# Last FFN: seven block products in group 10 as well, x added from DRAM onto the gated sum, adaLN tiles at a rate of each group until group 6, h of a group in one slot

## The chip, the cores and the metric

The kernel runs on one core of a Trainium2 chip. The metric is the time of one execution on the device in microseconds (us). Times of single instructions come from a hardware profile of one execution.

## What is computed

One residual block with three sublayers: an FFN at half weight, a mixer (mLSTM and RG-LRU heads), and a second FFN at half weight. Each has a modulation of its input and a gate that come from adaLN, the product of silu(c) and a weight matrix. The change lies in the third sublayer.

```python
def _swiglu(u, w13, w2):
    g, v = jnp.split(u @ w13, 2, axis=-1)
    return (jax.nn.silu(g) * v) @ w2
...
        mod = (jax.nn.silu(c) @ w_ada[l] + b_ada[l]).reshape(B, N_SUBLAYERS, 3, D_MODEL)
        shift, scale, gate = mod[:, :, 0], mod[:, :, 1], mod[:, :, 2]
...
        y = _swiglu(modulate(x, 2), ffn2_w13[l], ffn2_w2[l])
        x = _layer_norm(ALPHA * x + FFN_WEIGHT * gate[:, 2, None, :] * y, ln_g[l, 2], ln_b[l, 2])
```

x is 256 tokens by 2048 columns, the FFN is 5632 wide, everything is float32, and ALPHA is the fourth root of 2.

## The kernel before

**Weights.** Every weight tile is 128 partitions by 2048 columns, 1 MB, loaded by SyncE's queue into one of four raw buffers. `split` (called by `load_w`) makes a high half by a cast on ScalarE (ACT) and a low half by a subtraction on VectorE (DVE), line 110, three buffers each. A product is three passes: high by high, high by low, low by high. `mov_t` issues it for one tile and one half of the tokens as 12 matmuls of 128x512 on TensorE (PE), and `mov_w` for both halves, 24 matmuls.

**The last FFN** goes over 11 blocks of 512 columns of the FFN, 0 to 10. Blocks 0, 1 and 10 are made by `rows_block`: four weight tiles for g, four for v, 24 matmuls each. Blocks 2 to 9 (`FAST`) are made by `fast_block`: half of the inner dimension is taken with seven block products in place of eight, after Strassen and Winograd, from sums of the weight tiles that DVE makes (line 756, 761, 766 and 775) and from sums of the activations that `sums` makes once. Its 15 parts of 12 matmuls stand in place of 16. Between the parts it takes four `x_tile` steps, the products of the group before with w2, which are added to `yacc` by DVE (line 745). `turn_one` transposes the silu product of a block and makes its high and low half (h). `closing` makes the last w2 products and the last layer norm.

**x** is spilled to DRAM (`xd`) by `sums`, since its buffer is wanted for the sums of the activations. `restore` reads it back behind block 9 and multiplies it by ALPHA on ACT, and `residual` (lines 334 and 335) multiplies yacc by the gate and adds it onto x, on DVE, while block 10 runs.

**adaLN.** Every weight tile load calls `tick`, which adds a rate to a credit, and for each full credit one adaLN tile is loaded (1 MB into a raw buffer) and reduced by one operation on DVE, line 210. In the last FFN the rate is 0.5 and the credit starts at -2. Sixteen tiles, 128 to 143, give the gate of this sublayer; `gate_rows` turns them, writes them to DRAM and reads them back over all partitions with a DMA from GpSimd (POOL), line 234.

**Order.** A scheduler fixes the order of each engine's instructions when the program is built, and each engine takes its own in that order. An instruction waits until what it reads is there and the buffer that it writes is free, and everything behind it on its engine waits with it.

Names: the banks of a fast block are `fa`, `fb`, `fc` and `fd`; `py` is a bank for w2 products; `lfw` and `hfw` are the low and high halves of w13 tiles, `lw` and `hw` of w2 tiles; tile 20q is the second sum of block 2's tile 0 (a p, q or r behind the number marks a sum); `u` and `n` at the mixer's end are the modulated input of the last FFN, `tu` its transposed form, `sh`, `hf` and `lf` halves of its first weights.

Of the kernel before, what the change touches and what calls it, by code (L numbers as in the profile page):

```python
# [16 lines left out]
P = 128  # L17
# [24 lines left out]
FFN2_RATE = 0.5  # L42
# [3 lines left out]
FAST = range(2, 10)  # L46


class Held:
# [9 lines left out]
def block_kernel(ctx: ExitStack, tc: tile.TileContext, a: dict, out: bass.AP):  # L59
# [594 lines left out]
    def ffn(s, w13, w2, start, following=None):  # L654
# [8 lines left out]
        b0 = RAMP // 4 if start else 0  # L663
# [5 lines left out]
        def rows_block(b, passed=None):  # L669

            i = 8 * (b - b0)
            if passed:
                pg, pv = passed[0], met(passed, w13[4:8], f"fv{s}")
            else:
                pg = [bank(f"fg{s}{b}{t}") for t in range(NT)]
                for k in range(4):
# [4 lines left out]
                for k in range(4):
                    mov_w(pv, load_w(w13[i + 4 + k], f"fv{s}_{b}{k}"), uh, ul, k * 4, k == 0, k == 3)
# [5 lines left out]
        def sums():  # L688

            nc.gpsimd.dma_start(xd, x.tile)  # L690
            f = raw_tile("sums").rearrange("p (a b) -> p a b", b=P)
            for t in range(NT):
                tk = slice(t * P, (t + 1) * P)
                nc.vector.tensor_add(f[:, 8 * t:8 * t + 8, :], uh[:, 0:8, tk].bitcast(F32), ul[:, 0:8, tk].bitcast(F32))
            a11, a12, a21, a22 = (f[:, 4 * i:4 * i + 4, :] for i in range(4))
            nc.vector.tensor_add(a22, a21, a22)
            nc.vector.tensor_sub(a21, a11, a21)
            nc.vector.tensor_sub(a11, a22, a11)
            nc.vector.tensor_sub(a12, a12, a11)
            both = big.tile([P, 2, KT, P], F32R, tag="x", name="ws")  # L700
            nc.scalar.copy(both[:, 0], f)
            nc.vector.tensor_sub(both[:, 1], f, both[:, 0].bitcast(F32))
            return both[:, 0], both[:, 1]

        def restore():
            x.tile = tokens("x1")
            for t in range(NT):
                nc.gpsimd.dma_start(x[:, t, :], xd[:, t, :])
            scale_x()

        def fast_block(b, wh, wl):

            i = 8 * b
            gi = 4 * b // GRP - 1
            s2_, s4_, s3_, s1_ = 0, 4, 8, 12
            p1, p5 = bank(f"fa{b}"), bank(f"fb{b}")
            py = {}

            def part(ps, hl, h, k0, t, first, last):
                return mov_t(ps, hl, *h, k0, t, first, last, T, skip_group_check=not first and ps in (p1, p5))  # L720

            def fresh(k, row=False):
                return load(w13[i + k], f"fw{s}_{b}{k}", None, row_tile(f"fw{b}{k}") if row else None)

            def halves(tile, w=""):
                return split((tile[0], tile[1] + w, None), nc.scalar, nc.vector)

            def kept(ps, tag, w):
                to = sm.tile([P, 512], F32, tag=tag, bufs=2, name=f"{w}{s}{b}")
                nc.scalar.copy(to, ps)  # L730
                return to

            def x_tile(m):
                n, k = b % 2 * 2 + m // 2, m % 2
                if not k:
                    py[n] = [bank(f"py{gi}_{n}_{t}") for t in range(NT)]
                kg = 2 * gi + k
                end = mov_w(py[n], load_w(w2[kg * 4 + n], f"w2{s}_{kg}_{n}"), *hts[gi], k * 4, not k, k == 1, T)
                if k:
                    c = slice(n * 512, (n + 1) * 512)  # L740
                    for t in range(NT):
                        if gi == 0:
                            evac.append(nc.scalar.copy(yacc[t][:, c], py[n][t]))
                        else:
                            nc.vector.tensor_add(yacc[t][:, c], yacc[t][:, c], py[n][t])
                return end

            u, w = (uh, ul), (wh, wl)
            ta = fresh(0, True)
            end = part(p1, halves(ta), u, 0, 0, True, True)  # L750
            turn_one(end)
            f1 = kept(p1, "u", "fs")
            tc_ = fresh(4, b >= 4)
            end = x_tile(0)
            turn_one(end)
            nc.vector.tensor_sub(ta[0], tc_[0], ta[0])
            part(p5, halves(ta, "p"), w, s1_, 0, True, True)
            f5 = kept(p5, "gy", "ft")
# [337 lines left out]
        if not following:  # L1096
            return
# [461 lines left out]
```

## Time and profile before

| | us |
|---|---|
| median of 3 runs | 1883.9 |
| lowest and highest run | 1880.34, 1885.63 |
| the profiled execution | 1882.46 |
| its span | 1880.7 |
| PE busy | 1861.4 |
| DVE busy | 1561.3 |
| ACT busy | 895.1 |

The profile belongs to one execution, so that sums of its rows are to be set against 1882.46 and not against the median. Matmuls overlap: a row of PE gives 0.39 us for one, and the time from one start to the next is 0.23 us. A row of the timeline gives in brackets how long its engine stood idle ahead of the instruction, and what ended that. Group 10 of the title is block 10.

### The profile page before, as it was taken

The page shows a single profiled execution, that of the slowest core. Times are in us where ns is not written, and L with a number is a line of the kernel's source. Part 1 is how long each engine was busy: PE and PEld are TensorE (multiplying, and loading weights), DVE is VectorE, ACT ScalarE, POOL GpSimd, SP SyncE. Part 2 cuts the span into 40 slices and gives each one's busy share as a digit, 9 for nine tenths or more (in the row PEclk, how much of TensorE's full clock was granted, in tenths as well). Part 3 has the DMA queues.
Part 4 walks back from the last instruction along what each step waited for, and adds up shares of the span by engine and source line. Part 5 has one row for each costly group of instructions (what it writes and reads, how often), then busy time and mean ns, then how long its engine had stood idle before and what let it go on. Part 6 is the DMA issues. An engine that isn't in the chain of part 4 may idle for free.

```text
span 1880.7 us, 21240 instructions
## 1 busy us (share of the span) xinstructions
PE 1861.4 (99%) x8495; PEld 1526.0 (81%) x8495; DVE 1561.3 (83%) x1467; ACT 895.1 (48%) x847; POOL 43.2 (2%) x68
## 2 busy tenths in 40 slices
PE   8999999999999999999999999999999999999998
PEld 5788888888888888788888887878778888888886
DVE  6899998887887987889997877789887788778776
ACT  4543444533334335756644356454544455545441
POOL 0000000000000000100000121000000000000000
PEclk9999999999999999999999999999999999999999
DMA  9989889999899987478687574768855654564662
GB/s 377 417 354 366 319 311 347 357 348 355 344 357 355 339 331 269 148 276 296 244 317 296 203 264 182 268 246 300 307 210 190 224 212 168 202 224 186 239 224 90
DMA packets 74931, 520.06 MB, mean 277 GB/s; under 512 B 8736, under 2 KB 8912, under 8 KB 13520
## 3 DMA queue, kind: packets, MB, share of 16 engines
q1 hardware_dynamic: 72144, 507.54, 71.6%
q0 software_dynamic: 960, 7.37, 1.0%
q10 hardware_dynamic: 1728, 3.80, 0.6%
q8 instruction: 66, 1.08, 0.2%
q14 instruction: 33, 0.27, 0.0%
HBM read 514.46 MB, written 4.22 MB: 276 GB/s over the span
## 4 chain that ended last, share of the span: by engine, by line
PE 92%; DVE 4%; DMA 2%; issue 1%; ACT 1%; POOL 0%; POOLq 0%; DVEq 0%; SPq 0%; ACTq 0%
PE py L133 9%; PE pj L281 5%; PE fa L133 5%; PE fb L133 4%; PE fc L133 3%; PE fd L133 3%; PE py L293 3%; PE py L294 3%; PE py L292 3%; PE pj L283 3%; PE fg L293 3%; PE fg L294 3%; PE fg L292 3%; PE fv L293 3%; PE fv L292 3%; PE fv L294 3%
## 5 line engine op out<-in xcount | busy, mean ns | idle before, releaser
L210 DVE CUSTOM_DVE_ANT_0 ada<-ada,scb,badac 128x2048 f32<-128x2048 f32 x110 | 258.0, 2345 | 39.5 <-DMA ada<-in_w_ada 39.0
L108 ACT CAST hw<-rw 128x2048 fp32r<-128x2048 f32 x81 | 155.1, 1914 | 218.0 <-DMA rw<-in_w 60.6
L110 DVE TENSOR_TENSOR lw<-rw,hw 128x2048 fp32r<-128x2048 f32 x81 | 185.1, 2287 | 55.8 <-ACT hw L108 55.0
L110 DVE TENSOR_TENSOR lfw<-rfw,hfw 128x2048 fp32r<-128x2048 f32 x48 | 109.9, 2289 | 17.2 <-ACT hfw L108 17.2
L281 PE MATMUL pj<-u,hs 128*128 128x512 f32 x512 | 122.5, 391 | 0.0
L108 ACT CAST hra<-rra 128x2048 fp32r<-128x2048 f32 x38 | 72.6, 1914 | 102.2 <-DMA rra<-in_w_r 43.1
L108 ACT CAST hfw<-rfw 128x2048 fp32r<-128x2048 f32 x48 | 91.9, 1915 | 47.8 <-PE py L133 28.2
L281 PEld LDWEIGHTS pj<-u,hs 128*128 128x128 f32 x512 | 94.3, 188 | 18.4
L133 PE MATMUL py<-lw,hth 128*128 128x512 f32 x256 | 99.8, 390 | 2.1 <-DVE lw L110 2.1
L133 PE MATMUL py<-hw,hth 128*128 128x512 f32 x256 | 100.4, 392 | 0.0
L293 PE MATMUL py<-lw,hth 128*128 128x512 f32 x256 | 99.8, 390 | 0.1
L294 PE MATMUL py<-hw,htl 128*128 128x512 f32 x256 | 99.7, 390 | 0.0
L133 PE MATMUL py<-hw,htl 128*128 128x512 f32 x256 | 99.7, 389 | 0.0
L292 PE MATMUL py<-hw,hth 128*128 128x512 f32 x256 | 97.3, 392 | 0.0
L108 ACT CAST hfg<-rfg 128x2048 fp32r<-128x2048 f32 x28 | 53.6, 1914 | 86.1 <-DMA rfg<-in_w 48.8
L108 ACT CAST hs<-rs 128x2048 fp32r<-128x2048 f32 x32 | 61.0, 1908 | 68.7 <-PE pj L281 53.6
L293 PE MATMUL fg<-lfg,u 128*128 128x512 f32 x224 | 87.4, 390 | 0.1
L294 PE MATMUL fg<-hfg,u 128*128 128x512 f32 x224 | 87.3, 390 | 0.0
L293 PE MATMUL fv<-lfv,u 128*128 128x512 f32 x224 | 87.2, 389 | 0.0
L294 PE MATMUL fv<-hfv,u 128*128 128x512 f32 x224 | 87.1, 389 | 0.0
L108 ACT CAST hfv<-rfv 128x2048 fp32r<-128x2048 f32 x28 | 53.6, 1913 | 66.7 <-DMA rfv<-in_w 41.3
L292 PE MATMUL fg<-hfg,u 128*128 128x512 f32 x224 | 84.5, 392 | 0.0
(727 smaller groups left out, 4764.4 us busy)
## 6 DMA issues: line engine op xcount, KB each, us to landing
ada<-in_w_ada SPq DMA_DIRECT2D x138, 1024.0 KB, 6.5
rw<-in_w SPq DMA_DIRECT2D x81, 1024.0 KB, 5.5
rfw<-in_w SPq DMA_DIRECT2D x50, 1024.0 KB, 4.8
rra<-in_w_r SPq DMA_DIRECT2D x45, 1024.0 KB, 7.4
rs<-in_w_s SPq DMA_DIRECT2D x32, 1024.0 KB, 5.0
rfg<-in_w SPq DMA_DIRECT2D x28, 1024.0 KB, 6.7
rfv<-in_w SPq DMA_DIRECT2D x28, 1024.0 KB, 5.5
rwo<-in_w_out SPq DMA_DIRECT2D x16, 1024.0 KB, 4.8
```

The lines of the kernel that those rows point to most:

```text
L108: act.copy(cut(hi, w), like(raw[:, w], hi))
L110: low.tensor_sub(cut(lo, w), like(raw[:, w], lo), cut(hi, w).bitcast(F32))
L133: self.last = getattr(self.engine, op)(*args, **kw)
L210: vec.tensor_tensor_reduce(raw[:, c], raw[:, c], scb[:, c], 1.0, base, ALU.mult, ALU.add, to)
L281: nc.tensor.matmul(ps, hi[:, k * P:(k + 1) * P], both(k), start=k == 0, stop=False)
L283: nc.tensor.matmul(ps[:, 0:S], lo[:, k * P:(k + 1) * P], uh[:, k, :], start=False, stop=k == KT - 1)
L292: pe.matmul(o, acth[:, k0 + j, tk], cut(hi, w), start=first and j == 0, stop=False, **kw)
L293: pe.matmul(o, acth[:, k0 + j, tk], cut(lo, w), start=False, stop=False, **kw)
L294: end = pe.matmul(o, actl[:, k0 + j, tk], cut(hi, w), start=False, stop=last and j == 3, **kw)
```

## The change

`last_ffn` is a function of its own, and `ffn` serves the first FFN alone. In it:

- Blocks 2 to 10 are fast blocks. `fast_block` follows a plan, a list of steps: S4 for blocks 2 to 9, S2 for block 10, whose two w2 steps are the first two of the closing products. The signs of the sums are others, so that c - a, -a - d and a + b are made one after the other in the buffer of a, and c + d in that of c. In before a sum of b and a was made in the buffer of b.
- x is multiplied by ALPHA ahead of its spill. It isn't read back: when block 9 is done, yacc is multiplied by the gate in place, and two DMAs from POOL add xd onto yacc, which is x from there on.
- adaLN runs at a rate of its own for each block (0.5, 0.5, 0.17, 0.3, 0.3, 0.3 for blocks 0 to 5) from a credit of 0, and what is left is done ahead of block 6. From block 6 to 9 tile c takes a buffer of the two that the vector c of adaLN and the gate use; before it did from block 4 on.
- h is kept for each block in one slot, high and low half together; before, for each group of two blocks in two slots.

```diff
-FFN2_RATE = 0.5
+FFN2_RATE = (0.5, 0.5, 0.17, 0.3, 0.3, 0.3)
...
-FAST = range(2, 10)
...
+ADA_END = 6
...
-            credit[:] = -2.0, FFN2_RATE
-            rows_block(0, nxt.pop())
-            rows_block(1)
-            ws = sums()
-            for b in FAST:
-                fast_block(b, *ws)
-            restore()
-            done = FAST.stop // 2 - 1
...
+                elif w == "P5":
+                    W["c", q] = fresh(q, 4, not DOUBLE and ADA_END <= b < n_b - 1)
+                    a, c = W["a", q], W["c", q]
+                    vec.tensor_sub(a[0], c[0], a[0])
+                    hl = halves(a, "p")
...
+                elif w == "P6":
+                    a = W["a", q]
+                    d = W["d", q] = fresh(q, 5, q == 1)
+                    vec.scalar_tensor_tensor(a[0], a[0], -1.0, d[0], op0=ALU.mult, op1=ALU.subtract)
+                    hl = halves(a, "q")
...
+                elif w == "P7":
+                    c, d = W["c", q], W["d", q]
+                    if not dma:
+                        vec.tensor_add(c[0], c[0], d[0])
...
+                elif w == "P4":
+                    a = W["a", q]
+                    if not dma:
+                        vec.tensor_add(a[0], a[0], W["b", q][0])
+                    normal("4", halves(a, "r"), u, ku + 4, 1)
...
+        credit[:] = 0.0, FFN2_RATE[0]
+        rows_block(0, nxt.pop())
+        rows_block(1)
+        for t in range(NT):
+            nc.scalar.mul(x[:, t, :], x[:, t, :], ALPHA)
+        nc.gpsimd.dma_start(xd, x.tile)
+        ws = [sums(0, in_x)]
+        S4 = "P1 t X t P5 X P6 P3 X P7 P2 G P4 G X V".split()
+        S2 = "P1 t G t P5 X P6 P3 G P7 P2 X P4 V".split()
...
+        gate_rows(s, 0.5)
+        for t in range(NT):
+            for n in range(4):
+                c = slice(n * 512, (n + 1) * 512)
+                nc.vector.tensor_mul(yacc[t][:, c], yacc[t][:, c], gate[:, c])
+            nc.gpsimd.dma_start(yacc[t], xd[:, t, :], accum_op=ALU.add)
+        x.tile = yacc
...
+        fast_block(n_b - 1, ws[:1], begun(), S2)
```

**How it moves the order.** ACT at the end of the mixer, before: the modulated input (`u`, `n`) is made from its transposed form, token half 0.

```order
L133 ACTIVATE n_8253<-x_113,nbn_8250,rsn_8248 128x512
L133 ACTIVATE u_0_8273<-tu_0_8258,adac 128x128 x4
L133 ACTIVATE u_1_8300<-tu_1_8264,adac 128x128 x4
L133 CAST u_114<-u_1_8300 128x4x128
L133 ACTIVATE n_8253<-tu_2_8290,adac 128x128 x4
L133 ACTIVATE n_8253<-tu_3_8295,adac 128x128 x4
```

ACT at the same place in the change:

```order
L138 ACTIVATE n_8253<-x_113,nbn_8250,rsn_8248 128x512
L138 ACTIVATE u_0_8273<-tu_0_8258,adac 128x128 x4
L1164 ACTIVATE x_113<-x_113 128x2048
L138 ACTIVATE u_1_8300<-tu_1_8264,adac 128x128 x4
L138 CAST u_114<-u_1_8300 128x4x128
L138 ACTIVATE n_8253<-tu_2_8290,adac 128x128 x4
L138 ACTIVATE n_8253<-tu_3_8295,adac 128x128 x4
```

The multiplication of x's first half (L1164) stands between the two pieces of u; that of the second half stands in the same way ahead of the first piece of u for the second half.

DVE behind that, where the low half of the FFN's first weights is made (`lf`), before:

```order
L133 TENSOR_TENSOR u_114<-u_3_8470,u_114 128x4x128
L133 TENSOR_TENSOR lf_8496<-rf_8362,hf_8495 128x512 x4
L133 TENSOR_TENSOR u_114<-n_8253,u_114 128x4x128 x2
L110 TENSOR_TENSOR lfv2b_8541<-rfv2b_8538,hfv2b_8540 128x2048
L110 TENSOR_TENSOR lfv2b_8571<-rfv2b_8568,hfv2b_8570 128x2048
L110 TENSOR_TENSOR lfv2b_8601<-rfv2b_8598,hfv2b_8600 128x2048
L210 ISA ada_8705,adac<-ada_8705,scb,badac 128x2048
```

And in the change:

```order
L138 TENSOR_TENSOR u_114<-u_3_8470,u_114 128x4x128
L215 ISA ada_8566,adac<-ada_8566,scb,badac 128x2048
L215 ISA adac 128x1
L138 TENSOR_TENSOR lf_8496<-rf_8362,hf_8495 128x512 x4
L138 TENSOR_TENSOR u_114<-n_8253,u_114 128x4x128 x2
L115 TENSOR_TENSOR lfv2b_8539<-rfv2b_8536,hfv2b_8538 128x2048
L115 TENSOR_TENSOR lfv2b_8572<-rfv2b_8569,hfv2b_8571 128x2048
L215 ISA ada_8637,adac<-ada_8637,scb,badac 128x2048
```

The first adaLN operation (ISA ada) has moved ahead of `lf_8496`, and the second ahead of the third `lfv2b`.

DVE in block 3 from the low half of its second sum on, before:

```order
L110 TENSOR_TENSOR lfw_30q<-fw_9348,hfw_30q 128x2048
L110 TENSOR_TENSOR lfw_35_9498<-rfw_35_9441,hfw_35_9497 128x2048
L210 ISA ada_9566,adac<-ada_9566,scb,badac 128x2048
L210 ISA adac 128x1
L110 TENSOR_TENSOR lw_0_3_9518<-rw_0_3_9515,hw_0_3_9517 128x2048
L110 TENSOR_TENSOR lfw_34q<-rfw_34_9378,hfw_34q 128x2048
L110 TENSOR_TENSOR lfw_31_9572<-rfw_31_9569,hfw_31_9571 128x2048
L775 TENSOR_TENSOR rfw_31_9569<-rfw_31_9569,fw_9348 128x2048
```

And in the change:

```order
L115 TENSOR_TENSOR lfw_30q<-fw_30_9340,hfw_30q 128x2048
L115 TENSOR_TENSOR lfw_35_9490<-rfw_35_9468,hfw_35_9489 128x2048
L1132 TENSOR_TENSOR fw_30_9340<-fw_30_9340,rfw_31_9556 128x2048
L115 TENSOR_TENSOR lw_0_3_9510<-rw_0_3_9507,hw_0_3_9509 128x2048
L115 TENSOR_TENSOR lfw_34q<-rfw_34_9411,hfw_34q 128x2048
L115 TENSOR_TENSOR lfw_31_9559<-rfw_31_9556,hfw_31_9558 128x2048
L215 ISA ada_9623,adac<-ada_9623,scb,badac 128x2048
```

The adaLN operation has left the place ahead of the w2 tile `lw_0_3`, and the sum a + b (L1132), which was line 775 behind `lfw_31`, has come there.

DVE from the end of block 9 into block 10, before:

```order
L110 TENSOR_TENSOR lfw_97_12160<-rfw_97_12157,hfw_97_12159 128x2048
L745 TENSOR_TENSOR yacc_8509<-yacc_8509,py_3_0_11967 128x512
L745 TENSOR_TENSOR yacc_8510<-yacc_8510,py_3_1_11968 128x512
L110 TENSOR_TENSOR lfg_100_12256<-rfg_100_12253,hfg_100_12255 128x2048
L792 TENSOR_TENSOR fv_11949<-fv_11949,fb_11810 128x512
L793 TENSOR_TENSOR fs_11836<-fs_11836,fv_11949 128x512
L334 TENSOR_TENSOR gy_12227<-yacc_8509,gate_12225 128x512
L335 TENSOR_TENSOR x_12215<-x_12215,gy_12227 128x512
L334 TENSOR_TENSOR gy_12230<-yacc_8509,gate_12225 128x512
L335 TENSOR_TENSOR x_12215<-x_12215,gy_12230 128x512
```

And in the change:

```order
L115 TENSOR_TENSOR lfw_97_12161<-rfw_97_12158,hfw_97_12160 128x2048
L1035 TENSOR_TENSOR yacc_8954<-yacc_8954,py_3_0_11968 128x512
L1035 TENSOR_TENSOR yacc_8955<-yacc_8955,py_3_1_11969 128x512
L1188 TENSOR_TENSOR yacc_8954<-yacc_8954,gate_12221 128x512 x4
L1188 TENSOR_TENSOR yacc_8955<-yacc_8955,gate_12221 128x512 x4
L115 TENSOR_TENSOR lfw_100_12237<-fw_100_12233,hfw_100_12236 128x2048
L1148 TENSOR_TENSOR f_11950<-f_11950,f_11884 128x512
L1092 TENSOR_TENSOR fw_100_12233<-rfw_104_12301,fw_100_12233 128x2048
L1157 TENSOR_TENSOR f_11828<-f_11828,f_11950 128x512
L115 TENSOR_TENSOR lfw_102_12265<-rfw_102_12262,hfw_102_12264 128x2048
L1149 TENSOR_TENSOR f_11897<-f_11897,f_11811 128x512
L1121 TENSOR_TENSOR rfw_104_12301<-rfw_104_12301,rfw_105_12355 128x2048
```

The eight products by the gate stand in a row ahead of the low half of block 10's first tile, and two sums of weight tiles (L1092, L1121) follow.

## Rows read from the trace of the kernel before

**Rows 1.** The page, part 1: busy time, share of the span and instructions of each engine.

```profile
PE 1861.4 (99%) x8495; PEld 1526.0 (81%) x8495; DVE 1561.3 (83%) x1467; ACT 895.1 (48%) x847; POOL 43.2 (2%) x68
```

**Rows 2.** What PE waits for, 1230 to 1881: us in total, times, longest.

```profile
PE fa L133 <- DVE lfw_20q L110: 2.6, 1, 2.6
PE py L133 <- DVE lw L110: 2.1, 2, 1.3
```

**Rows 3.** Busy time by stretch; columns in the first line.

```profile
core 0: us, PE busy (x) PEld busy (x) DVE busy (x) ACT busy (x) POOL busy (x), PEclk, DMA share, GB/s
1242.00:1300.00 58.00, 55.42 (x241) 45.06 (x240) 51.38 (x33) 30.58 (x24) 0.00 (x0) 0.97 0.74 274
...
1509.00:1576.00 67.00, 67.00 (x301) 55.50 (x300) 53.99 (x35) 34.75 (x26) 0.00 (x0) 1.00 0.55 201
```

**Rows 4.** Timeline of PE: start, duration, engine, line, instruction, [idle before, releaser].

```profile
1257.78 0.39 PE L133 MATMUL py<-hw,htl 128*128 128x512 f32 x1
...
1260.05 0.39 PE L133 MATMUL fa<-hfw_20q,ws 128*128 128x512 f32 x1
1263.02 0.50 PE L133 MATMUL fa<-lfw_20q,ws 128*128 128x512 f32 x1 [2.58 <-DVE lfw_20q L110]
...
1267.16 0.47 PE L133 MATMUL fb<-hfw,ws 128*128 128x512 f32 x1
...
1324.44 0.50 PE L133 MATMUL py<-lw,hth 128*128 128x512 f32 x1 [0.77 <-DVE lw L110]
```

**Rows 5.** Busy time around the wait at 1263; columns as in rows 3.

```profile
1262.50:1267.20 4.70, 4.18 (x12) 3.27 (x13) 4.70 (x3) 0.13 (x1) 0.00 (x0) 0.65 0.68 234
```

**Rows 6.** Timeline of ACT, the two multiplications of x.

```profile
1745.59 3.71 ACT L133 ACTIVATE x<-x 128x2048 f32<-128x2048 f32 x2
```

**Rows 7.** Timeline of ACT at the end of the mixer.

```profile
1149.64 2.90 ACT L133 ACTIVATE u<-tu,adac 128x128 f32<-128x128 f32 x8 [0.47 <-PE tu L133]
1152.58 0.62 ACT L133 CAST u<-u 128x512 fp32r<-128x512 f32 x1
...
1162.81 1.50 ACT L133 ACTIVATE u<-tu,adac 128x128 f32<-128x128 f32 x4 [0.43 <-PE tu L133]
1164.35 0.62 ACT L133 CAST u<-u 128x512 fp32r<-128x512 f32 x1
```

**Rows 8.** Timeline of PE at the end of the mixer.

```profile
1153.25 0.50 PE L133 MATMUL f<-sh,u 128*128 128x512 f32 x1
...
1165.56 0.47 PE L133 MATMUL f<-hf,u 128*128 128x512 f32 x1
...
1177.00 0.39 PE L293 MATMUL f<-lf,u 128*128 128x512 f32 x1
```

**Rows 9.** Timeline of DVE: an adaLN operation, and lf.

```profile
1258.40 2.35 DVE L210 CUSTOM_DVE_ANT_0 ada<-ada,scb,badac 128x2048 f32<-128x2048 f32 x1 [2.08 <-DMA ada<-in_w_ada]
...
1175.43 2.49 DVE L133 TENSOR_TENSOR lf<-rf,hf 128x512 fp32r<-128x512 f32 x4
```

**Rows 10.** Timeline of DVE from the end of block 9 on.

```profile
1747.93 1.35 DVE L745 TENSOR_TENSOR yacc<-yacc,py 128x512 f32<-128x512 f32 x2
...
1762.15 2.28 DVE L110 TENSOR_TENSOR lfg<-rfg,hfg 128x2048 fp32r<-128x2048 f32 x1
1764.36 0.68 DVE L335 TENSOR_TENSOR x<-x,gy 128x512 f32<-128x512 f32 x1
1764.96 0.68 DVE L793 TENSOR_TENSOR fu<-fu,ft 128x512 f32<-128x512 f32 x1
```

**Rows 11.** DMA issues, 1130 to 1881: KB each, median us to landing.

```profile
xd<-x POOLq DMA_DIRECT2D x1, 2048.0 KB, 11.1
...
gate<-rowd POOLq DMA_DIRECT2D x1, 1024.0 KB, 8.3
```

**Rows 12.** Busy time in block 10; columns as in rows 3.

```profile
1759.28:1802.80 43.52, 43.52 (x197) 36.08 (x196) 31.91 (x30) 19.17 (x13) 0.00 (x0) 1.00 0.54 194
```

**Rows 13.** Timeline of POOL, the gate's transfer.

```profile
1742.98 0.56 POOL L234 DMA_DIRECT2D gate<-rowd  x1 [5.26 <-DVE lfw L110]
```

More of the change, by code (lines that the diff above doesn't have):

```diff
@@ L54, in __getitem__ @@
     def __getitem__(self, key):
+        if isinstance(self.tile, list):
+            p, t, c = key
+            return self.tile[t][p, c]
         return self.tile[key]
@@ L662, in ffn @@
         evac = []
-        b0 = RAMP // 4 if start else 0
+        b0 = RAMP // 4
         sts = new_stats(s)
@@ L686, in rows_block @@
                 swiglu(b, t, pg[t], pv[t])
[L688 to L758, printed above, removed]
-            td = fresh(5)
-            x_tile(1)
-            nc.vector.tensor_sub(ta[0], td[0], ta[0])
-            part(p1, halves(ta, "q"), w, s2_, 0, False, True)
-            f2 = kept(p1, "gy", "fv")
-            part(p5, halves(td), w, s4_, 0, False, False)
-            x_tile(2)
-            nc.vector.tensor_sub(tc_[0], td[0], tc_[0])
-            part(p1, halves(tc_, "q"), w, s3_, 0, False, True)
-            f3 = kept(p1, "u", "fu")
-            p2, p4 = bank(f"fc{b}"), bank(f"fd{b}")
-            tb = fresh(1)
-            part(p2, halves(tb), u, 4, 0, True, False)
-            g2_ = load_w(w13[i + 2], f"fw{s}_{b}2")
-            part(p2, g2_, u, 8, 0, False, False)
-            part(p4, g2_, u, 8, 1, True, False)
-            nc.vector.tensor_sub(tb[0], tb[0], ta[0])
-            part(p4, halves(tb, "p"), u, 4, 1, False, False)
-            g3_ = load_w(w13[i + 3], f"fw{s}_{b}3")
-            part(p2, g3_, u, 12, 0, False, True)
-            part(p4, g3_, u, 12, 1, False, True)
-            nc.vector.tensor_add(f1, f1, p2)
-            nc.scalar.activation(f1, f1, AF.Silu)
-            nc.vector.tensor_add(f3, f3, p4)
-            nc.scalar.activation(f3, f3, AF.Silu)
-            x_tile(3)
-            vs = [load_w(w13[i + 4 + k], f"fw{s}_{b}{4 + k}") for k in (2, 3)]
-            for t, ps in enumerate((p5, p1)):
-                for k in range(2):
-                    part(ps, vs[k], u, 8 + 4 * k, t, False, k == 1)
-            if 4 * b // GRP not in hts:
-                new_h(4 * b // GRP)
-            for t, h, v, ps in ((0, f1, f2, p5), (1, f3, f5, p1)):
-                nc.vector.tensor_add(v, v, ps)
-                nc.vector.tensor_mul(h, h, v)
-                to_turn.append((b, t, h))
@@ L973, in g1 @@
             grp = groups[gi]
-            if start and gi == 2:
+            if gi == 2:
                 new_h(gi)
@@ L982, in g1 @@
                 return
-            if start and gi == 3:
+            if gi == 3:
                 for t in range(NT):
@@ L1083, in ffn @@
                 credit[0] -= 2.0
-            if gi == len(groups) - 1 and following:
+            if gi == len(groups) - 1:
                 credit[:] = 0.0, 0.0
                 g2_kept(gi - 1)
-            elif gi == len(groups) - 1:
-                closing(gi)
-            elif gi:
-                if start:
-                    g2(gi - 1)
+            else:
+                g2(gi - 1)
                 if gi == len(groups) - 2:
```

288 lines of the change are left out of this document (232 added, 56 removed).

## The prediction

> **What bounds the kernel now.** I read the page's engine line first [rows 1]: TensorE (PE) is busy 99% of the span, so only two things move the time: the number of matmuls, and the few places where PE waits. The change lies in the last FFN, so I then asked what PE waits for from 1230 us to the end [rows 2]: 2.6 us once for the low half of tile 20q, and 2.1 us in two pieces, the longer 1.3, for low halves of w2 tiles. The stretches show where [rows 3]: PE is short of its stretch by 2.58 us in 1242 to 1300 and by nothing in 1509 to 1576, where VectorE (DVE) still has 13.0 us free in 67. So the FFN is bound by PE alone from 1442 us on. Ahead of that, DVE is late, because it makes the low half of each weight tile and also runs the adaLN tiles. The wait at 1263 costs more than its 2.58 us: the twelve matmuls behind it end at 1267.16, 4.14 us after they began, where ten matmuls before it took 2.27 us (1257.78 to 1260.05), so twelve should take 2.72 [rows 4]. The granted clock of 1262.5 to 1267.2 is 0.65 [rows 5], a mix of the two levels 2.4 and 1.2 GHz. That is 1.42 us more. Waits of the kernel before that the change can touch: 2.58 + 1.42 + 2.1 = 6.1 us.
>
> **Block 10 with seven products.** Its first half takes 15 parts of 12 matmuls instead of 8 tiles of 24: 180 for 192. At the 0.227 us of [rows 4] that is 12 x 0.227 = -2.7 us on PE, all of it on the path if PE doesn't wait. Nothing else on PE is added or removed in number.
>
> **x times ALPHA, moved to the boundary.** Two ScalarE (ACT) multiplications of 128x2048 go from 1745.59, where they took 3.71 us for both [rows 6] in ACT's free time, to the mixer's end. There ACT is on the path, and PE waits for it at once [rows 7, 8]. u_0 and u_1 are eight activations in a row from 1149.64 to 1152.54, their cast ends at 1153.20, and PE's matmul on sh starts at 1153.25, 0.05 us later. The first multiplication now stands between u_0 and u_1: start to start 1.85 us, so PE waits +1.8 us. The second stands ahead of u11_0. ACT there was idle 0.43 us before 1162.81, so 1.85 - 0.43 = 1.4 us come through, PE had 0.6 us to spare (the cast ends at 1164.97, PE goes at 1165.56), so +0.8 us. Nothing hides these two; they would be free only if the scheduler's order differed.
>
> **The first adaLN tile, ahead of lf.** The rate now starts at a credit of 0 instead of -2, and tile 128 stands on DVE ahead of the four subtractions that make the low half lf_8496; before, it stood five rows later. An adaLN operation takes 2.35 us [rows 9]. lf's four pieces take 2.49 us from 1175.43 [rows 9], so the first is ready at 1176.1, and PE takes it at 1177.00 [rows 8], 0.9 us later. DVE's start moves with ACT by about 3.1 us, PE by the 2.6 us above, so lf's first piece comes at 1176.1 + 3.1 + 2.35 = 1181.5 and is wanted at 1179.6: +1.9 us. Together the boundary costs +4.5 us. Bounds: +2 if the second and third hide each other, +6.5 if one gap of about 2 us also drops the clock as at 1263, where that cost 1.42.
>
> **The accumulating DMAs, and x not read back.** Before, two reads of x from DRAM and eight pairs of product and sum on DVE; now eight products by the gate in place and two GpSimd DMAs that add. DVE saves eight sums of 0.60 us start to start [rows 10]. The DMAs are wanted only in the closing part, more than 60 us after their issue, and two large POOL transfers of the trace take 8.3 and 11.1 us [rows 11]; an adding one isn't shown, and even at 30 us it costs nothing by itself. I take 0 for it, and no gain, since nothing waits for it earlier. That h now lies in one slot for each block leaves its casts and subtractions as many as before: 0.
>
> **adaLN at a rate for each group.** Before, eleven adaLN tiles fall in blocks 2 and 3 of DVE's order, now six, with three in block 4 and one in block 5. The one at 1258.40 started 2.08 us after DVE came free, since its transfer landed late [rows 9], and the low half of 20q stood behind it. That place is gone. In its stead, from block 2 on, the sum for the seventh product's last operand (a += b) stands ahead of the low half of the second w2 tile of the third X step; before, the corresponding sum stood after the low half of b. It costs 2.20 us, the start-to-start time of a low half [rows 10], and waits for b's transfer. In block 3 an adaLN tile stood in the same place and PE waited 0.77 us for lw at 1324.44 [rows 4], so I take 1.0 to 1.5 us there, 0.3 to 1.0 in blocks 4 and 5 that still have adaLN, and 0.1 in each of blocks 6 to 9, where DVE has its 13 us [rows 3]. Sum after about 2.2 us, against 6.1 before: -3.9 us. Bounds: after from 1 to 6 us, so -5.1 to -0.1.
>
> **Block 10 and the gate.** This is the place where DVE becomes tight. Block 10 had 31.9 us of DVE in 43.5 of PE [rows 12]. Now PE has 180 + 48 matmuls x 0.227 = 51.7 us. DVE has 13 low halves x 2.20 = 28.6, four combinations of weights x 2.20 = 8.8, eight products by the gate x 0.60 = 4.9, four more on w2 = 2.4 with a low half of 2.2, and some twelve small ones = 7: about 54 us, of which 4 may run before the block. The gate's products stand between the yacc sums of block 9 and the low half of tile 100. The gate's DMA shares its buffer with a weight tile of block 9 and is issued when that is read, at 1742.98 [rows 13]; it takes 8.3 us [rows 11], so it lands at 1751.3. The yacc sums end at 1749.28 [rows 10], so DVE waits 2 us, does the eight products until about 1756.7 (with some 0.6 us added for a later issue), then the low half of 100 until 1758.9, just in time for block 10's first matmul at 1759.28. Then come f2, c - a, f1 and the low half of 102: 0.6 + 2.2 + 0.6 + 2.2 = 5.6, until 1764.5, and PE wants it after P1 and a few transposes, at about 1762.8: +1.7 us. Three more of the same kind follow while DVE is behind: +0.4 at the second transposed half, +0.5 at 100q, +1.2 at 103 behind a += b. Sum +3.8 us. Bounds: +1, if DVE starts with the gate there, to +7, if the gate lands 3 us later, which goes through one to one.
>
> A rule speaks against the row here. The gate's 1 MB took 8.3 us from issue to landing [rows 11]. The Trainium skill, DMA: Bandwidth & Descriptors, Anatomy of one DMA - SWDGE (gpsimd) path, gives 2.0 us plus bytes over 436e3 for a GpSimd transfer, an estimate of 4.4 us for 1 MB. By it the products would begin 2 us earlier and the block would cost some 2 us less, +1.8 instead of +3.8. I keep the row, since the same transfer stands in this kernel.
>
> **The sum.** +4.5 - 3.9 - 2.7 + 3.8 = +1.7 us. The profiled execution took 1882.5 us, the median of the runs is 1883.9; on the first this gives 1884.2, on the second 1885.6. I say 1885. A measurement of this kernel tells apart about 0.3%, 5.6 us, so the forecast is no change that can be told.
>
> **Rivals.** (A) Faster: the boundary's gaps hide one another (+2), the waits in blocks 2 to 9 fall to 0.3 (-5.8), and block 10 costs +1, with the -2.7. That is -5.5 us, 1878.4 at the median. For it: DVE's 13 us of free time in each block, and 0 waits in blocks 5 to 9 before. Against: the first boundary gap has a margin of 0.05 us, and block 10 has no spare DVE time. Going beyond 0.3% needs a little more than this.
> (B) Slower: a += b ahead of lw. It holds lw back in every block, not only in block 3, if b's transfer lands later than DVE reaches the sum. Its price is the 0.77 us that an operation in that place cost in block 3 [rows 4], or more: at 0.9 in each of eight blocks 7.2 us instead of 2.2, so +6.7 in all, 1890.6. It decides from about 0.8 us in each block. Against it: b is loaded ahead, and ACT and DVE are free for much of a block.
> (C) The change doesn't do what it says: the adaLN tiles find other places to be late in, and the stalls of blocks 2 to 5 stay at 6.1 us: +4.5 + 0 - 2.7 + 3.8 = +5.6, 1889.5. For it: ten of the sixteen still run in blocks 2 to 5.
> A wait as long as that at 1263 took the granted clock down and cost 1.42 us more [rows 4, 5]; only one wait of the sum, that on lf, comes near it, so the sum holds no such term and the upper bound does.
>
> **How the numbers follow.** The forecast 0.60; A 0.21; B 0.11; C 0.08. A lies at the edge, so of A and the forecast's lower tail I put 0.21 beyond -0.3%; half of C and all of B, with a tail of the forecast, give 0.15 beyond +0.3%; the rest, 0.64, within. The bounds of the terms summed give -4.8 to +10.7 at the extremes, and not all are reached together: 1877 to 1892 holds 8 in 10.
>
> **What would show it.** In the changed kernel's waits of PE: a gap of 1.8 us at the matmul on sh near 1153, one of about 2 us on lf near 1180; at most 3 us in blocks 2 to 9, none of it on tile 20q; and low halves of 102, 100q and 103 as what PE waits for in block 10. If block 10 shows no waits, the DVE walk is wrong; if the boundary has none, the order on ACT was not what bound it; if lw is waited for in blocks 6 to 9, B decides.

## The result and the profile after

The changed kernel takes 1888.5 us (median of 15 runs, 1882.4 to 1894.6) against 1883.4 of the kernel before (15 runs, 1880.2 to 1885.9): ratio 1.0027, interval 1.0016 to 1.0039, that is 5.1 us or 0.27% slower. The forecast was no change that can be told, 1885. The profiled execution took 1889.6, with a span of 1887.8.

The page of the changed kernel, part 1, answers to [rows 1]:

```profile
PE 1863.0 (99%) x8483; PEld 1524.8 (81%) x8483; DVE 1572.5 (83%) x1470; ACT 902.4 (48%) x854; POOL 43.8 (2%) x68
```

PE has twelve matmuls fewer, and its busy time is even so 1.6 us longer, in part because matmuls ran at a lower clock in two stretches of 10 us (30 to 40 and 1250 to 1260, granted clock 0.83), where the kernel before has one (1260 to 1270, 0.83). What PE waits for from 1140 us on answers to [rows 2]; columns as there:

```profile
PE th L972 <- DVE sg L956: 3.5, 1, 3.5
PE py L138 <- DVE lw L115: 2.3, 2, 1.5
PE f L138 <- ACT u L138: 1.8, 2, 1.6
PE f L298 <- DVE lf L138: 1.7, 1, 1.7
PE f L138 <- DVE lfw L115: 0.9, 1, 0.9
PE f L138 <- DVE lfw_40q L115: 0.8, 1, 0.8
...
PE f L138 <- DVE lfw_100q L115: 0.3, 1, 0.3
```

The rows left out are two waits that both kernels have, 0.4 us on u and 0.8 in the closing part. In time order the waits of the change are: 1.64 us at 1156.74 and 0.17 at 1169.49 for ACT's u (boundary), 1.69 at 1182.92 for lf (boundary), 3.49 at 1255.17 for a silu product (sg) of block 1, 0.83 at 1341.57 and 1.47 at 1471.88 for a w2 tile (blocks 3 and 5), 0.77 at 1400.69 for 40q (block 4), and 0.25 and 0.86 in block 10.

In this one execution the change is 7.2 us behind before at the end of the last w2 product (1876.90 against 1869.72). Of these, 1.7 us lie ahead of the boundary, at a matmul that started at 1152.11 and in [rows 8]'s kernel at 1150.42; none of the eleven other kernels below, which share that part, shows them (1150.3 to 1150.7). They are lost near the start of this execution, with columns as in [rows 3]:

```profile
30.00:40.00 10.00, 8.09 (x15) 3.15 (x14) 4.88 (x8) 4.58 (x7) 0.00 (x0) 0.83 1.02 421
```

The granted clock is 0.83 there and 1.00 in the same stretch of the kernel before, and 10 us at 0.83 lose 10 x 0.17 = 1.7 us. So 5.5 us belong to the change, near the 5.1 of the medians.

The boundary. ACT's timeline, which answers to [rows 7]: the first multiplication of x stands between the two pieces of u.

```profile
1151.34 1.50 ACT L138 ACTIVATE u<-tu,adac 128x128 f32<-128x128 f32 x4 [0.47 <-PE tu L138]
1152.72 1.92 ACT L1164 ACTIVATE x<-x 128x2048 f32<-128x2048 f32 x1
1154.53 1.51 ACT L138 ACTIVATE u<-tu,adac 128x128 f32<-128x128 f32 x4
1156.07 0.62 ACT L138 CAST u<-u 128x512 fp32r<-128x512 f32 x1
```

DVE's timeline a little later, which answers to [rows 9]: the adaLN operation ends at 1182.2, and lf begins only there.

```profile
1179.90 2.35 DVE L215 CUSTOM_DVE_ANT_0 ada<-ada,scb,badac 128x2048 f32<-128x2048 f32 x1
...
1182.17 2.50 DVE L138 TENSOR_TENSOR lf<-rf,hf 128x512 fp32r<-128x512 f32 x4
```

The new wait in block 2. DVE's timeline around it, with L1121 the sum c += d and L956 the silu products of block 1:

```profile
1239.92 2.35 DVE L215 CUSTOM_DVE_ANT_0 ada<-ada,scb,badac 128x2048 f32<-128x2048 f32 x1 [0.57 <-DMA ada<-in_w_ada]
...
1244.52 2.29 DVE L1092 TENSOR_TENSOR fw<-rfw,fw 128x2048 f32<-128x2048 f32 x1
1250.02 2.29 DVE L1121 TENSOR_TENSOR rfw<-rfw,rfw 128x2048 f32<-128x2048 f32 x1 [3.21 <-DMA rfw<-in_w]
1252.23 2.28 DVE L115 TENSOR_TENSOR lw<-rw,hw 128x2048 fp32r<-128x2048 f32 x1
1254.43 1.28 DVE L956 TENSOR_TENSOR sg<-sg,fv 128x512 f32<-128x512 f32 x2
```

DVE stands idle for 3.21 us until d's transfer lands, and the low half of a w2 tile and both products stand behind it; PE has nothing to do until the first of them is there. The transfers' issues on SyncE's queue show why d came late:

```profile
1234.98 0.33 SPq L211 DMA_DIRECT2D ada<-in_w_ada  x1
1237.18 0.33 SPq L103 DMA_DIRECT2D rfw<-in_w  x1
...
1242.31 0.33 SPq L103 DMA_DIRECT2D rfw<-in_w  x1
```

The adaLN tile issued at 1234.98 holds one of the four raw buffers until its operation ends at 1242.20; d's transfer is issued at 1242.31 and lands 7.7 us later. PE behind the wait:

```profile
1255.17 0.66 PE L972 MATMUL th<-ident,sg 128*128 128x128 f32 x4 [3.49 <-DVE sg L956]
1255.58 0.47 PE L138 MATMUL py<-hw,ht 128*128 128x512 f32 x1
...
1259.77 0.40 PE L138 MATMUL py<-hw,ht 128*128 128x512 f32 x1
```

From 1255.58 to 1259.77 are 11 matmuls in 4.19 us where 11 at full clock take 2.49 (11 x 0.227): 1.7 us more. The granted clock of 1249 to 1262 is 0.87.

Block 10. The gate's transfer on POOL, which answers to [rows 13], and the products on DVE:

```profile
1744.66 0.52 POOL L236 DMA_DIRECT2D rowd<-grow  x1 [576.33 <-ACT grow L235]
1749.11 0.56 POOL L239 DMA_DIRECT2D gate<-rowd  x1 [3.93 <-DMA rowd<-grow]
```

```profile
1757.59 4.91 DVE L1188 TENSOR_TENSOR yacc<-yacc,gate 128x512 f32<-128x512 f32 x8 [0.85 <-DMA gate<-rowd]
1762.41 2.28 DVE L115 TENSOR_TENSOR lfw<-fw,hfw 128x2048 fp32r<-128x2048 f32 x1
...
1768.02 2.29 DVE L115 TENSOR_TENSOR lfw<-rfw,hfw 128x2048 fp32r<-128x2048 f32 x1
...
1782.95 2.29 DVE L115 TENSOR_TENSOR lfw_100q<-fw,hfw_100q 128x2048 fp32r<-128x2048 f32 x1 [1.43 <-ACT hfw_100q L113]
...
1789.56 2.29 DVE L115 TENSOR_TENSOR lfw<-rfw,hfw 128x2048 fp32r<-128x2048 f32 x1
```

The eight products by the gate take 4.8 us and end at 1762.4. Block 10's first matmul is at 1766.73. The low half of 102 ends at 1770.3, and PE's step of 24 matmuls on it takes 6.15 us (1769.82 to 1775.97) instead of 5.44, of which 0.25 is a gap at its end, ahead of the transposition of the second silu product (that is ready at 1775.90); the step on 100q takes 3.28 instead of 2.72, and the two steps on 105 and 103 9.36 instead of 8.16. With 0.1 more at P5 that is 2.6 us, of which the view of waits shows 1.1 in rows of their own.

### The profile page after: what moved, and what is told of

Same layout as the page of the kernel before. It is cut to its first block, busy times and chain, and to the rows that moved or that the text cites. A ratio compares the mean times of both kernels' runs of the same rounds, so it can differ in the third digit from the quotient of the medians.

```text
span 1887.8 us, 21251 instructions
## 1 busy us (share of the span) xinstructions
PE 1863.0 (99%) x8483; PEld 1524.8 (81%) x8483; DVE 1572.5 (83%) x1470; ACT 902.4 (48%) x854; POOL 43.8 (2%) x68
## 5 line engine op out<-in xcount | busy, mean ns | idle before, releaser
L138 PE MATMUL f<-hfw,u 128*128 128x512 f32 x720 | 226.6, 389 | 0.0
L138 PE MATMUL py<-hw,ht 128*128 128x512 f32 x512 | 164.9, 393 | 0.0
L138 PEld LDWEIGHTS f<-hfw,u 128*128 128x128 f32 x720 | 135.1, 188 | 28.0
L138 PE MATMUL f<-lfw,u 128*128 128x512 f32 x360 | 140.3, 390 | 0.9 <-DVE lfw L115 0.9
L138 PEld LDWEIGHTS py<-hw,ht 128*128 128x128 f32 x512 | 96.8, 189 | 20.1
L138 PE MATMUL py<-lw,ht 128*128 128x512 f32 x256 | 100.5, 393 | 2.3 <-DVE lw L115 2.3
L298 PE MATMUL py<-lw,hth 128*128 128x512 f32 x256 | 99.8, 390 | 0.1
L299 PE MATMUL py<-hw,htl 128*128 128x512 f32 x256 | 99.7, 390 | 0.0
L297 PE MATMUL py<-hw,hth 128*128 128x512 f32 x256 | 97.3, 392 | 0.0
L138 DVE CUSTOM_DVE_ANT_0 ada<-ada,scb,badac 128x2048 f32<-128x2048 f32 (+1 forms) x34 | 73.3, 2157 | 2.9 <-DMA ada<-in_w_ada 2.6
```

The lines of the kernel that those rows point to most:

```text
L138: self.last = getattr(self.engine, op)(*args, **kw)
L297: pe.matmul(o, acth[:, k0 + j, tk], cut(hi, w), start=first and j == 0, stop=False, **kw)
L298: pe.matmul(o, acth[:, k0 + j, tk], cut(lo, w), start=False, stop=False, **kw)
L299: end = pe.matmul(o, actl[:, k0 + j, tk], cut(hi, w), start=False, stop=last and j == 3, **kw)
```

## The experiments

Each is timed in five rounds beside the kernel before on the same chip, so the ratios to before are to be compared. The changed kernel has 1.0027. By the intervals of the ratios, a difference between two kernels is known to almost 3 us each way, so small ones are read from the traces.

**The credit.** The adaLN credit starts at -2 as before.

```diff
-        credit[:] = 0.0, FFN2_RATE[0]
+        credit[:] = -2.0, FFN2_RATE[0]
```

> The changed kernel with the credit of the last FFN started at -2 again, as before, and nothing else: the adaLN operations come two tiles later, so none stands ahead of the low half lf, one still stands ahead of block 2. Theory (boundary cost is the x multiplications plus the adaLN operation ahead of lf; block 2's wait is c += d): PE's 1.69 us wait on lf is gone, the wait near 1255 of 3.5 us stays, the two tiles pushed into block 5 cost 0 to 1 us there, so 1 to 2 us faster than the changed kernel, ratio to before about 1.002. Rival (the adaLN rate made the wait in block 2): that wait goes as well, 5 us faster than the changed kernel, ratio about 1.000.

Measured: 0.9996 (0.9988 to 1.0005), 1881.7 us. The wait on lf is gone, that near 1255 stays, and it is 2.16 us here instead of 3.49. So it is 5.8 us faster than the change by the ratios, three times what the theory had. Profile against profile it is 4.2 us: 1.7 is the wait on lf, 1.3 the shorter wait in block 2, 1.7 the early stretch at the lower clock that only the change's execution has, less 0.5 more at 40q. The rival's number came, but not its mechanism, since the wait it wanted gone is there, and DVE's and SyncE's order in block 2 is that of the change. The profiled execution took 1885.4, 3.7 above the median, so a usual one may have less of these waits. In the four profiles that show the wait in block 2 (the change, this kernel, and below block 10 with eight tiles and a += b held back), it is 3.49, 2.16, 2.21 and 4.61 us; d's transfer takes 7.2 to 7.7 us in all of them. What moves is the adaLN operation whose buffer d wants: in the three with the credit of 0 it starts 57.0, 56.1 and 58.7 us behind the matmul on lf.

**x off the boundary.** As above, and the two multiplications behind block 0's silu.

```diff
-        for t in range(NT):
-            nc.scalar.mul(x[:, t, :], x[:, t, :], ALPHA)
+        with tc.issue_after(made_sg[1].ins):
+            for t in range(NT):
+                nc.scalar.mul(x[:, t, :], x[:, t, :], ALPHA)
```

> As e2_credit, and the two ACT multiplications of x by ALPHA are held back behind the last silu of block 0, off the boundary. Theory: the waits of 1.64 and 0.17 us on ACT's u at the boundary are gone too, so about 2 us faster than e2_credit; here the scheduler also puts one of the two silu products of block 1 ahead of c += d on DVE, so that if c += d is what PE waited for near 1255, that wait goes as well and the sum is 5 to 7 us below the changed kernel, ratio to before 0.999 to 1.000. Rival (PE at the boundary is held by something else, such as the transfer of weights): within 1 us of e2_credit.

Measured: 0.9980 (0.9970 to 0.9989), 1879.2 us. Both waits for ACT's u are gone, and so is that near 1255. One of the products now stands ahead of c += d, but c += d itself doesn't wait any more (it starts at 1242.95; the adaLN operation ran earlier, at 1231.15, and d was issued at 1235.73), so this kernel doesn't tell the place of the sum from the lateness of d. It is 8.9 us faster than the change by the ratios, where the theory had 5 to 7. The waits that are left:

```profile
PE f L138 <- DVE lfw_40q L115: 3.0, 1, 3.0
PE py L138 <- DVE lw L115: 2.6, 3, 1.4
PE f L138 <- DVE lfw L115: 0.9, 1, 0.9
```

In block 4 an adaLN operation that waits 3.76 us for its transfer holds back 40q by 3.0 us, where the kernel with the old credit had 1.2. The waits that went are 1.64 + 0.17 + 2.16 = 4.0 us, those that came 2.0; the medians differ by 2.5, the ratios by 3.0. The profiled execution took 1882.7, 3.4 above its median; that the wait in block 4 is shorter in most executions is likely, but not shown.

**c += d held back in every block**, behind the low half of sum q (`last_low` is the low half issued last).

```diff
                     hl = halves(a, "q")
+                    held = last_low[0]
...
                     if not dma:
-                        vec.tensor_add(c[0], c[0], d[0])
+                        with tc.issue_after(held.ins):
+                            vec.tensor_add(c[0], c[0], d[0])
```

> The changed kernel with the sum c += d of each fast block held back on DVE behind the low half of the second sum (q) of its block; SP's order and the rest are the same. Theory (c += d waits for d's transfer, and the silu products of block 1 stand behind it): the 3.5 us wait near 1255 and about 1.7 us of halved clock behind it go, 4 to 5 us faster than the changed kernel, ratio to before 1.000. Rival (d's late transfer, which waits for the raw buffer of an adaLN tile, is the cause whoever stands behind it): PE waits 2 to 3 us for d's product or the sum q some microseconds later instead, and the gain is under 2 us.

Measured: 1.0019 (1.0010 to 1.0028), 1887.0 us; the runs lie within 1.6 us, those of the change within 12. The wait near 1255 is gone, as the theory had it, but only 1.5 us are gained. PE's waits:

```profile
PE py L139 <- DVE ht L976: 3.3, 4, 0.8
PE f L139 <- DVE lfw L116: 2.2, 2, 1.4
PE py L139 <- DVE lw L116: 2.2, 4, 1.0
PE f L139 <- ACT u L139: 1.8, 2, 1.6
PE f L299 <- DVE lf L139: 1.7, 1, 1.7
...
PE th L973 <- DVE f L1160: 0.6, 1, 0.6
```

In blocks 2, 4, 6 and 8 PE now waits 0.8 us for the low half of h (`ht`), in the odd blocks 0.3 to 1.0 for the w2 tile, and in block 10 0.8 for 105 and 1.4 for 103, where the change has 0.9 on 103: the sum and what the scheduler placed around it has taken another place ahead of something wanted. The theory on the cause stands, the edit was too broad. The rival's place (sum q, or d's product) shows no wait in blocks 2 to 9; the 0.8 for 105 in block 10 is one at d's product.

**All three.** 

> All three together: credit from -2, x multiplied behind block 0's silu, c += d held back. Theory: the boundary's 3.5 us and block 2's 5.2 us go, the waits of blocks 3 to 5 (3.1 us) and of block 10 (2.6 us) stay or move: 7 to 9 us faster than the changed kernel, ratio to before 0.997 to 0.999. Rival (waits are a matter of transfers in total and move on): 3 us faster than the changed kernel, ratio 1.001.

Measured: 0.9999 (0.9991 to 1.0008), 1882.9 us, within 1.1 us of each other. The boundary's waits are gone, and those of c += d held back in every block are there but for one of 0.6 us. It is 5.3 us faster than the change by the ratios, short of the theory's 7 to 9. By the medians it is 3.6 us slower than the kernel that lacks only that edit: there the wait in block 2 was gone already, and what the hold adds is 0.8 us in each of blocks 2, 4, 6 and 8, 0.4 in 7 and 9 and 1.1 in block 10. In blocks 3 to 5 it takes waits away (0.5 each in 3 and 5, and the 3.0 us at 40q).

**c += d held back in block 2 alone**, behind the silu products of block 1.

```diff
-                        vec.tensor_add(c[0], c[0], d[0])
+                        with tc.issue_after(last_mul[0].ins) if b == 2 else nullcontext():
+                            vec.tensor_add(c[0], c[0], d[0])
```

> The changed kernel with c += d held back in block 2 alone, and only behind the silu products of block 1; SP's order is the same. Theory (only those two small products behind c += d matter): the wait of 3.5 us near 1255 and its halved clock go, nothing comes in their place in blocks 6 to 9, so 4 to 6 us faster than the changed kernel, ratio to before 0.9995 to 1.0005, and the spread of its runs falls from 12 us to about 5. Rival (d's late transfer costs its time anyhow): a wait of 2 to 3 us at the sum q of block 2 or at d's product, gain under 2 us, spread as wide as before.

Measured: 0.9996 (0.9987 to 1.0005), 1882.8 us, 5.8 us faster than the change; the runs lie within 3.7 us. SyncE's order is the same as in the change. DVE around the place that showed the wait:

```profile
1241.33 2.29 DVE L1093 TENSOR_TENSOR fw<-rfw,fw 128x2048 f32<-128x2048 f32 x1
1243.94 2.29 DVE L115 TENSOR_TENSOR lw<-rw,hw 128x2048 fp32r<-128x2048 f32 x1 [0.32 <-ACT hw L113]
1246.15 0.68 DVE L957 TENSOR_TENSOR sg<-sg,fv 128x512 f32<-128x512 f32 x1
1247.43 0.69 DVE L957 TENSOR_TENSOR sg<-sg,fv 128x512 f32<-128x512 f32 x1 [0.60 <-PE fv L299]
1248.04 2.29 DVE L1123 TENSOR_TENSOR rfw<-rfw,rfw 128x2048 f32<-128x2048 f32 x1
```

The products are ready at 1248.1, c += d follows without a wait since d has landed by then, and PE waits nowhere between 1181 and 1334. From the matmul on lf to the wait for a w2 tile in block 3 are 158.65 us in the change:

```profile
1182.92 0.50 PE L298 MATMUL f<-lf,u 128*128 128x512 f32 x1 [1.69 <-DVE lf L138]
...
1341.57 0.50 PE L138 MATMUL py<-lw,ht 128*128 128x512 f32 x1 [0.83 <-DVE lw L115]
```

Here they are 153.35 us:

```profile
1181.34 0.50 PE L298 MATMUL f<-lf,u 128*128 128x512 f32 x1 [1.69 <-DVE lf L138]
...
1334.69 0.50 PE L138 MATMUL py<-lw,ht 128*128 128x512 f32 x1 [0.86 <-DVE lw L115]
```

This is the experiment that tells what makes the wait in block 2: with the same transfers in the same order, the place of one sum in DVE's order is worth 5.3 us in these two executions, and nothing comes in its stead. That it is all of the loss can't be said: the old credit (above) and a += b held back (below) gain as much by the ratios, 5.8 and 5.5 us, and leave that wait where it is.

**Block 10 with eight tiles.**

```diff
-        fast_block(n_b - 1, ws[:1], begun(), S2)
+        rows_block(n_b - 1)
+        for end in begun():
+            turn_one(end)
```

> The changed kernel with block 10 made by eight tiles of 24 matmuls as before, the two w2 steps behind it; the gated sum in place and the adding DMAs stay. Theory (seven products save 12 matmuls, 2.7 us, and DVE's queue of that block gives 2.6 us back): PE's waits in block 10 go and 12 matmuls come, so within 1.5 us of the changed kernel, ratio to before 1.002 to 1.0035, PE's waits at low halves 100q and 103 gone from the profile. Rival (the eight products by the gate in a row are what makes DVE late, whatever block 10 does): PE still waits 2 us and the kernel is 2 to 3 us slower than the changed one, ratio 1.004.

Measured: 1.0022 (1.0013 to 1.0031), 1887.5 us: 1 us faster than the change with seven, inside both intervals. PE waits nowhere in block 10. The traces tell it closer: from the wait for a w2 tile in block 5 to the first matmul behind the last w2 product are 405.5 us here and 405.3 in the change. So what seven products save there, DVE gives back but for 0.3 us, as the sum had it. In block 4 this execution has a wait of 1.32 us that the change's hasn't: c += d waits 2.66 us for d there as well, ahead of a w2 tile. So the same sum can be late in another block in another execution.

**a += b held back** behind the low half of the tile ahead of it in the plan.

```diff
                     c, d = W["c", q], W["d", q]
+                    held = last_low[0]
...
-                        vec.tensor_add(a[0], a[0], W["b", q][0])
+                        with tc.issue_after(held.ins):
+                            vec.tensor_add(a[0], a[0], W["b", q][0])
```

> The changed kernel with a += b held back behind the low half of the weight tile that stands ahead of it in the plan (lw of the third w2 step, or tile 103 in block 10). Theory: the waits for lw in blocks 3 (0.8) and 5 (1.5) go, and that of 0.9 to 1.2 us at 103 in block 10, so 2 to 3 us faster than the changed kernel, ratio to before 1.001 to 1.002; the wait near 1255 stays. Rival (a += b is then late for its own product, as c += d held back was for others): as many waits at tile a's last sum, within 1 us of the changed kernel.

Measured: 0.9998 (0.9989 to 1.0006), 1882.9 us, 5.5 us faster than the change, more than the 2 to 3 expected. The waits for the w2 tile in blocks 3 and 5 and that at 103 are gone (0.83 + 1.47 + 1.2 = 3.5 us by the profile of the change), a wait of 0.2 has come, and none for tile a's last sum. PE's waits there and near 1255:

```profile
PE th L972 <- DVE sg L956: 4.6, 1, 4.6
...
PE py L138 <- DVE lw L115: 0.2, 1, 0.2
```

That near 1255 is 4.61 us in the profiled execution, the slowest of the eleven. That the gain is 2 us above the removed waits stays open; the difference of the ratios isn't known closer than that.

**The four holds together**: credit, x, c += d in block 2, a += b.

> Credit from -2, x multiplied behind block 0's silu, c += d behind the silu products in block 2, a += b behind the tile ahead of it. Theory: what is left is a late adaLN tile in block 4 (1 to 3 us) and 1 to 1.5 us in block 10, so 9 to 12 us faster than the changed kernel, ratio to before 0.9965 to 0.998. Rival (the waits move on): as e12_x_late_credit, ratio 0.998 to 0.999.

Measured: 0.9951 (0.9939 to 0.9963), 1874.2 us, 9.4 us faster than before by the medians and 14 than the change by the ratios, more than the 9 to 12 expected. The gains of the single steps (5.8, 3.0, 5.8 and 5.5 us) add up to 20, so they overlap or are partly noise, and none of them is to be read as the price of its wait alone. PE's waits:

```profile
PE f L138 <- DVE lfw_40q L115: 0.9, 1, 0.9
...
PE f L138 <- DVE lfw_100q L115: 0.2, 1, 0.2
```

**Block 10 with eight tiles, on top of these.** The edit is that of the other kernel with eight tiles.

> c57 with block 10 made by eight tiles of 24 matmuls. Theory (seven products save 2.7 us of matmuls, and DVE gives back about 1 us of it in c57): 1 to 2.5 us slower than c57, ratio to before 0.9957 to 0.9965. Rival (the saved matmuls are hidden behind DVE in any case): within 0.7 us of c57.

Measured: 0.9960 (0.9948 to 0.9973), 1876.5 us, 2.2 us slower than with seven by the medians, 1.7 by the ratios. By the traces it is 1.6 us (475.2 against 473.7 from the wait at 40q to the first matmul behind the last w2 product), where it was 0.3 in the change. So with a += b out of the way, seven products are worth 1.6 to 2.2 of their 2.7 us.

**The gate's row written two blocks earlier.** The write to DRAM stands ahead of block 8, the read back where it was.

```diff
             if b == ADA_END:
                 ada_until(s, 2, KT - 1)
+            if b == 8:
+                gate_rows(s, 0.5)
...
-        gate_rows(s, 0.5)
+        gate_back(s)
```

> c57 with the gate's values written to DRAM two blocks earlier, so that its transfer back waits only for its buffer; six of the eight products by the gate then stand in block 9 on DVE. Theory (block 10's waits come from the gate's products that hold DVE back): the waits at 102 and 100q of block 10, some 1 us in c57, go, 0.5 to 1.5 us faster than c57, ratio to before 0.9943 to 0.9948. Rival (block 10's DVE queue itself is too long): within 0.5 us of c57, PE still waits at 100q.

Measured: 0.9943 (0.9931 to 0.9956), 1873.4 us, the fastest here: 9.3 us below before by the medians, 0.8 below the kernel without this edit. That is inside the intervals; by the traces the stretch from 40q to the end of the w2 products is 1.2 us shorter (472.5 against 473.7). The issue of the gate's transfer on POOL:

```profile
1603.98 0.52 POOL L236 DMA_DIRECT2D rowd<-grow  x1 [417.21 <-ACT grow L235]
1715.98 0.56 POOL L244 DMA_DIRECT2D gate<-rowd  x1 [111.48 <-DVE lfw_94q L115]
```

It now waits for its buffer (the low half of 94q) and is issued at 1715.98, 37 us ahead of block 10's first matmul instead of 17.6. Block 10 has no wait left.

**The old rate.** The adaLN rate of before, with the rest of the change.

```diff
-        credit[:] = 0.0, FFN2_RATE[0]
+        credit[:] = -2.0, 0.5
...
-                    credit[1] = FFN2_RATE[b + i] if b < ADA_END else 0.0
+                    credit[1] = 0.5
```

> The changed kernel with the adaLN rate of before (0.5 throughout, credit from -2), the rest as changed. Theory (the rate of each group takes adaLN tiles out of blocks 2 and 3, but the credit of 0 costs 1.7 us at lf, and the wait near 1255 is c += d): no wait on lf; eleven adaLN operations in blocks 2 and 3, which make PE wait 4 to 8 us there, now from late adaLN transfers; within 3 us of the changed kernel, ratio to before 1.001 to 1.004. Rival (the new rates themselves are the loss): 4 us or more faster than the changed kernel, ratio 1.000 or below.

Measured: 1.0005 (0.9996 to 1.0014), 1884.4 us: 4.1 us faster than the change, between the two. PE waits 0.5, 1.2, 2.1 and 1.4 us in blocks 2 to 4, 5.2 in all, against 6.6 in the change, and the granted clock falls to 0.83 once in both (here behind the wait of 2.1, from 1330 to 1340). But other adaLN tiles gave DVE another order too, in which c += d stands behind the products. So what the rates alone are worth can't be read from it and stays open.

## Why the prediction came out as it did

**Block 10, matmuls and DVE.** Forecast -2.7 + 3.8, measured -2.7 + 2.6. The places were those named: 102 (1.7 forecast, 0.5 measured), the second transposed half (0.4 and 0.25), 100q (0.5 and 0.6), 103 (1.2 and 1.2). 102 was less late since the gate's products ended 4.3 us ahead of block 10's first matmul, not 2.5. That seven products gain next to nothing until DVE is freed is shown by both kernels with eight tiles (0.3 and 1.6 us by the traces). One point of the working was wrong: in the change the gate's transfer waits for the row's own write to DRAM (3.93 us on POOL), not for its buffer, and writing the row early shows what that and the products' place cost, 0.8 us by the medians and 1.2 by the traces.

**The rule weighed there.** The Trainium skill, DMA: Bandwidth & Descriptors, Anatomy of one DMA - SWDGE (gpsimd) path, gives 4.4 us for 1 MB by its fit, an estimate. The trace of the changed kernel disagrees as that of before did: from 1749.11 to the first product at 1757.59 are 8.5 us.

**The boundary.** Forecast +4.5, measured 1.64 + 0.17 + 1.69 = 3.5 in waits, and 4.2 by the times of the matmul on lf (1177.00 to 1182.92 is 5.9, less 1.7 from ahead of it). The first multiplication and lf were right to 0.2; the second came through with 0.2 instead of 0.8. Both causes are shown: the wait on lf goes with the old credit, and those on u with x moved.

**Adding DMAs.** Forecast 0, and no row waits for them. They are issued at 1760.6 and 1763.0 and take 9.8 us.

**Blocks 2 to 9.** This step failed: -3.9 forecast, about +2 measured (waits after 3.49 + 1.70 of clock + 0.83 + 0.77 + 1.47 = 8.3). The 6.1 before were a little too low: behind the wait at 1263 stand eleven matmuls and not twelve, since the first of that step went ahead of the wait at 1260.05, so the clock cost 4.14 - 11 x 0.227 = 1.64 us and the sum is 6.3. By the times, from the matmul on lf to block 10's first are 582.3 us before and 583.8 after, +1.5. Blocks 3 to 5 were near: 2.2 forecast, 3.1 measured, for lw behind a += b in 3 and 5 as named, while block 4's wait was at 40q behind an adaLN tile, which wasn't named. In 6 to 9 there was none. What was missing is block 2, which the sum had at nothing. The prediction said that the place of 20q is gone and looked no further for another operation in the same block that waits for a transfer; c += d is one, placed ahead of block 1's products. The bound for the step, 6 us after, was too low by 2.3. With that one sum held back the wait and the lower clock behind it are gone, 5.3 us by the traces, and the kernel is as fast as before (0.9996).

**The total** was 1.7 forecast, and 5.1 measured, because of 5.2 us in block 2 that were not in the sum, less 1.0 at the boundary and 1.2 in block 10 that were too much in it, and 0.9 more in blocks 3 to 5 (5.6 by these rows, 5.5 in the profiled execution). So the range held, and by the 0.3% of the text the change is no change that can be told, though the interval of fifteen runs lies above 1. That it came out so is luck in good part: the largest term of the result was in none of the sums, and terms that were too high at the boundary and in block 10 made up for 2.2 of its 5.2 us. Rival (B) named the mechanism, a sum of weights that waits ahead of something that PE wants, but at another sum, in another place: a += b cost 2.3 us in two blocks, not 0.9 in eight. (C) came nearest, with 1889.5 for stalls that find another place, though the adaLN tile had its part only as the holder of d's buffer. The times suggest that: d is issued 0.1 us behind the end of that operation, and where the operation ran earlier (x off the boundary) d was there in time. No run isolates it.

## What to carry to other kernels

Where a scheduler fixes the order, look at each operation of the busy engine that waits for a transfer, and at what stands behind it, above all at the operations of the stage before: one sum placed ahead of two products of 0.6 us cost 5.3 us in the profiled execution. When such a sum is to be moved, move it in the block where it hurts: the same hold in every block gave most of the gain back in waits of 0.3 to 1.4 us. A saving on the bounding engine counts only when the next engine has time in that very stage, and the transfer that a new in-place product waits for should be issued as early as its buffer allows (0.8 to 1.2 us here).

## What the hardware showed that was not expected

The length of a wait, as the rows give it, doesn't tell whether the clock falls behind it: in the kernel with the old credit a wait of 2.16 us was followed by a granted clock of 0.87 from 1249 to 1262, and in that with eight tiles in block 10 a wait of 2.21 us at the same place left it at 1.00:

```profile
1249.00:1262.00 13.00, 11.52 (x48) 9.43 (x49) 11.06 (x8) 5.30 (x7) 0.00 (x0) 0.87 0.43 161
```

```profile
1249.00:1262.00 13.00, 10.79 (x52) 8.66 (x51) 12.67 (x9) 6.07 (x7) 0.00 (x0) 1.00 0.33 110
```

The columns are those of [rows 3]. And the spread of the runs differs more than the medians: 12 us in the change (15 runs), 5.7 in the kernel before (15), 5.9, 4.7 and 6.6 in three that keep the wait in block 2 (the old credit, a += b held back, block 10 with eight tiles; 11, 11 and 12), 3.7 with c += d held back in block 2 (11), 1.6 with it held back everywhere (11), 0.8 in the kernel with all four holds (5). Waits that hang on a transfer would widen it so, but that isn't shown: the numbers of runs differ, and the three kernels that keep the wait spread about half as far as the change.
